# Two gated-DeltaNet heads through one blockwise inverse, in the same tiles and banks

## The chip, the cores and the metric

The kernel runs on one core of a Trainium2 chip. The metric is device time in microseconds (us) of that core, from the start of the program to its end; a time is the median of several executions. A core has a matrix engine (TensorE, PE in the profile, with its weight loads as PEld), a vector engine (VectorE, DVE), a scalar engine (ScalarE, ACT), a general one (GpSimd, POOL) and a queue that issues the DMAs (SyncE, SP). Each takes its instructions in the order in which the program holds them and stops at the first that is not ready.

## What is computed

Two decoder layers over x of shape (1, 512, 1024). Each layer is `x += norm(mixer(norm(x)))`, then `x += norm(ffn(norm(x)))`. The mixer of layer 0 has an mLSTM with 4 heads and a gated DeltaNet (GDN) with 4 heads beside each other; the change touches only the GDN heads. For one head, in chunks of 64 tokens:

```python
kk = jnp.einsum("nbhld,nbhsd->nbhls", kc, kc)
a_mat = jnp.where(strict, bc[..., :, None] * kk * decay, 0.0) + jnp.eye(L)
rhs = jnp.concatenate([vc * bc[..., None], kc * (bc * jnp.exp(G))[..., None]], -1)
sol = lax.linalg.triangular_solve(a_mat, rhs, left_side=True, lower=True, unit_diagonal=True)
u, w = sol[..., :DV], sol[..., DV:]
attn = jnp.einsum("nbhld,nbhsd->nbhls", qc, kc) * decay
def step(state, inp):
    v_new = u_ - w_ @ state
    o = qd_ @ state + attn_ @ v_new
    state = gl_ * state + kd_.T @ v_new
```

q and k are the l2-normed outputs of a depthwise convolution with SiLU on a projection of u, v the same without the norm; the output goes through a norm per head and a gate.

## The kernel before

The 512 tokens stand as four tiles of 128. A matrix product in about full fp32 precision is three matmuls of fp32r halves (`mm3`, lines L188 to L190: high by high, high by low, low by high). A projection of 128 features (`feature_block`) is 8 x 3 such matmuls of 128x512 into one PSUM bank, called pf; a token block (pt) has 256 columns. The weights of a block come by one DMA (raw) and are split into whi (a cast on ACT) and wlo (a subtraction, L101, on DVE or POOL).

PSUM has eight banks, in four groups: pj (3, the projections), mx (2, all the small work of the heads), sc (2, the scans) and po (1). A tile that asks for a bank waits until the last reader of the tile before in that bank is done.

A GDN head (`gdn_head`) runs so. `decay_t` broadcasts a row over the partitions (rowbc) and makes dec; qd is the decayed q. The keys are transposed (kt), ACT squares them with an accumulated sum (`chunk_squares`, L420) for the l2 norm, and DVE makes kbe and kd. Then mt = -(k k^T) times decay and beta, in four tiles of 128x128 (L682). The chunk of 64 tokens gives two 64-row halves of each tile, so that with the four tiles there are eight triangular matrices; the inverse works on the two halves as two 64x64 quadrants of TensorE (`both`). It builds X and its transpose xt from blocks of 1, 2, 4, up to 64 rows: a first run of matmuls (pp, pq, L716 and L717) with a fill for blocks of 2; five levels, each a run of pp (L734), a copy of it to PR on ACT (L736), a run of pe and pet (L740, L741) and two fills on DVE (`copy_predicated`, L708); and a last run (pp, pq, L748, L751, a copy of PR, L753, and pd, L758). ACT puts the result into xtf. After that come wt = kbe times the inverse (L764), the transposes of q (qt) with their squares for the norm of the queries (nq), the scan over the four tiles (vn, S, o) and the head's output (`head_out`). at = k q^T stands behind the first fills, the transposes of v (vt) ahead of level 32.

The heads are called as gdn(0), gdn(1), mlstm(0), gdn(2), gdn(3), mlstm(1); each mlstm takes two heads. Before a head its blocks k, q, v and gate are projected, and the next head's blocks are what TensorE has to do while a chain of small steps is under way. The order on each engine is not that of the code: at build a list scheduler lays all instructions out by modelled costs and writes one fixed sequence for each engine. The program therefore has small steps of a head with projection matmuls (pf, pt) between them.

Of the kernel before, what the change touches and what calls it, by code (L numbers as in the profile page):

```python
# [8 lines left out]
AF = mybir.ActivationFunctionType  # L9
# [9 lines left out]
P = 128  # L19
S = 512  # L20
# [15 lines left out]
def kernel(  # L36
# [409 lines left out]
    def ab_mix(pm, u, load0, pre):  # L446
        w_in = ab_w_in[0]
        wv = w_in.rearrange("(k p) c -> p k c", p=P)
        BUFS = dict(dm=1, mt=1, X=1, PR=1, wt=1, vb=1, v=1, kbe=1, dec=3)
# [21 lines left out]
        gw = small("gw", [P, KD, 16])  # L471
# [31 lines left out]
        first = [piece(fcols(c, 0), V) for c in (2056, 1544, 2568)]  # L503
# [40 lines left out]
        xtfs = [small(f"xtf{i}", [P, S]) for i in range(2)]  # L544
        for x_ in xtfs:
            G.memset(x_, 0.0)

# [12 lines left out]
        e = small("e", [P, NT, 8])  # L560
        stt(e, pf, -1.0, pf, ALU.mult, ALU.max)
        A.activation(out=e, in_=e, func=AF.Exp, scale=-1.0)
        z = small("z", [P, NT, 8])
# [3 lines left out]
        z2 = small("z2", [P, NT, 8])  # L567
        tt(V, z2, z, z, ALU.mult)
        hn = small("hn", [P, NT, 8])
# [81 lines left out]
        def gdn_head(h, k, q, vf, gs):  # L651
            dec, prow = decay_t(4 + h, bg[:, :, 4 + h], True)
            qd = s("qd")
            A.activation(out=qd, in_=prow, func=AF.Exp)
            gl = small("gl", [P, NT], bufs=2)
            V.tensor_copy(gl, v4(qd)[:, :, P - 1])
            tt(V, qd, qd, q, ALU.mult)
            pt = mxt("kt")
            transpose4(pt, k, range(NT))
            ss = col(4, "l2s")  # L660
            chunk_squares(ss, v4(pt))
            v = col(4, "l2v")
            V.tensor_scalar(out=v, in0=ss, scalar1=0.5, scalar2=EPS / 2, op0=ALU.mult, op1=ALU.add)
            rk = rsqrt(v, 4, "l2")
# [3 lines left out]
            ik = col(4, "ik")  # L668
            stt(ik, v, 2.0, rk, ALU.mult, ALU.mult)
            r2 = col(4, "r2")  # L670
            tt(V, r2, rk, rk, ALU.mult)
            dr = small("dr", [P, NT], bufs=2)
            tt(V, dr, r2, beta[:, :, h], ALU.mult)
            dm = s("dm")
            stt(v4(dm), v4(dec), -1.0, bc(dr, P), ALU.mult, ALU.mult)
            kbe = s("kbe")
            tt(V, v4(kbe), v4(pt), bc(eg[:, :, h], P), ALU.mult)
            kd = s("kd")
            tt(V, v4(kd), v4(pt), bc(v4(dec)[:, :, P - 1], P), ALU.mult)
            pmt = mxt("mt")  # L680
            for cs in css:
                T.matmul(pmt[:, cs], lhsT=k[:, cs], rhs=k[:, cs], start=True, stop=True)  # L682

            mt = s("mt")
            tt(V, mt, pmt, dm, ALU.mult)
# [3 lines left out]
            lo, hi = slice(0, 64), slice(64, P)  # L689
            both = ((lo, lo, hi), (hi, hi, lo))  # L690
            xt, xx = (small(n, [P, NT, 64]) for n in ("xt", "X"))
            for x_ in (xt, xx):
                A.copy(out=x_, in_=bm(identc, NT))

            def fill(b, x_, data, t, rows=slice(0, P)):

                def part(ap):
                    return ap.rearrange("p c (n a r) -> p c n a r", a=2, r=b)[:, :, :, t, :]

                if t:  # L700
                    mask = mkt[rows, LEVELS.index(b), :].rearrange("p (n r) -> p n r", r=b)
                elif b == 1:
                    mask = mk1[rows].rearrange("p (n r) -> p n r", r=1)
                else:
                    mask = mk[rows, LEVELS.index(b) - 1, :].rearrange("p (n a r) -> p n a r", a=2, r=b)[:, :, 0, :]
                n = 32 // b
                mask = mask.unsqueeze(1).broadcast_to([mask.shape[0], NT, n, b])
                V.copy_predicated(out=part(x_), mask=mask, data=part(data))  # L708

            def halves_of(ps):  # L710
                return ps[:, : NT * 64].rearrange("p (c n) -> p c n", c=NT)

            pp, pq = (halves_of(mxt(n)) for n in ("pp", "pq"))
            for c in range(NT):
                for rs, cs, os in both:
                    T.matmul(pp[rs, c], lhsT=v4(mt)[rs, c, cs], rhs=identc[rs], start=True, stop=True)  # L716
# [3 lines left out]
            pa = mxt("at")  # L720
            for cs in css:
                T.matmul(pa[:, cs], lhsT=k[:, cs], rhs=q[:, cs], start=True, stop=True)
            at_ = dec
            tt(V, at_, pa, dec, ALU.mult)
            for b in LEVELS[1:-1]:
                if b == 32:
                    pt = mxt("vt")
                    transpose4(pt, vf, range(NT))
                    vb = s("vb")
                    tt(V, v4(vb), v4(pt), bc(ik, P), ALU.mult)  # L730
                pp = halves_of(mxt("pp"))
                for c in range(NT):
                    for rs, cs, os in both:
                        T.matmul(pp[os, c], lhsT=v4(mt)[rs, c, cs], rhs=xx[rs, c], start=True, stop=True)  # L734
                pr = small("PR", [P, NT, 64])
                A.copy(out=pr, in_=pp)  # L736
                pes = [halves_of(mxt(n)) for n in ("pe", "pet")]
                for c in range(NT):
                    for rs, _, os in both:
                        T.matmul(pes[0][rs, c], lhsT=xt[os, c], rhs=pr[os, c], start=True, stop=True)  # L740
                        T.matmul(pes[1][os, c], lhsT=pr[os, c], rhs=xt[os, c], start=True, stop=True)  # L741
                fill(b, xx, pes[0], 0)
                fill(b, xt, pes[1], 1)

            xtf = xtfs[h % 2]
            pp, pq = (halves_of(mxt(n)) for n in ("pp", "pq"))
            for c in range(NT):
                T.matmul(pp[lo, c], lhsT=v4(mt)[lo, c, hi], rhs=xx[lo, c], start=True, stop=True)  # L748
            for c in range(NT):
                for rs, _, os in both:  # L750
                    T.matmul(pq[rs, c], lhsT=identc[os], rhs=xt[os, c], start=True, stop=True)  # L751
            pr = small("PR", [P, NT, 64])
            A.copy(out=pr[lo], in_=pp[lo])  # L753
            for rs, cs, _ in both:
                A.copy(out=v4(xtf)[rs, :, cs], in_=pq[rs])
            pd = halves_of(mxt("pd"))
            for c in range(NT):
                T.matmul(pd[lo, c], lhsT=pr[lo, c], rhs=xt[lo, c], start=True, stop=True)  # L758
            A.copy(out=v4(xtf)[lo, :, hi], in_=pd[lo])
            xt = xtf  # L760

            pw = mxt("wt")
            for cs in css:
                T.matmul(pw[:, cs], lhsT=kbe[:, cs], rhs=xt[:, cs], start=True, stop=True)  # L764
            wt = s("wt")
            A.copy(out=wt, in_=pw)
            pt = mxt("qt")
            transpose4(pt, q, range(NT))

            nq = col(4, "nq")  # L770
            chunk_squares(nq, v4(pt))
            V.tensor_scalar(out=nq, in0=nq, scalar1=EPS, scalar2=0.5 * P * EPS, op0=ALU.add, op1=ALU.mult)

            st = None
            po = bank("po", "o")
            for c, cs in enumerate(css):
                pn = bank("sc", "vn")
                T.matmul(pn[:, :P], lhsT=xt[:, cs], rhs=vb[:, cs], start=True, stop=c == 0)
                if c:
# [470 lines left out]
```

## Time and profile before

| | |
|---|---|
| median of 3 runs | 1356.19 us (1356.08 to 1356.34) |
| the profiled execution | 1356.14 us, span 1354.4 us |
| granted clock of TensorE | 0.998 |
| busy share of the span | PE 98%, PEld 80%, DVE 50%, ACT 45%, POOL 27% |
| DMA | 121.26 MB, mean 90 GB/s |

The span is the time between the first and the last instruction that the profiler recorded. A row of the timeline reads: start, length, engine, line of the kernel, operation, output tile<-input tiles, shape, count, and in brackets the idle time ahead with what ended it. The length of a matmul's row contains the depth of the pipeline, so the rows overlap; what a matmul costs in a sequence is the distance from its start to the start of the next. A matmul on plain fp32 that isn't a transpose has two records (16 records of pp are 8 matmuls).

### The profile page before, as it was taken

The page shows a single profiled execution, that of the slowest core. Times are in us where ns is not written, and L with a number is a line of the kernel's source. Part 1 is how long each engine was busy: PE and PEld are TensorE (multiplying, and loading weights), DVE is VectorE, ACT ScalarE, POOL GpSimd, SP SyncE. Part 2 cuts the span into 40 slices and gives each one's busy share as a digit, 9 for nine tenths or more (in the row PEclk, how much of TensorE's full clock was granted, in tenths as well). Part 3 has the DMA queues.
Part 4 walks back from the last instruction along what each step waited for, and adds up shares of the span by engine and source line. Part 5 has one row for each costly group of instructions (what it writes and reads, how often), then busy time and mean ns, then how long its engine had stood idle before and what let it go on. Part 6 is the DMA issues. An engine that isn't in the chain of part 4 may idle for free.

```text
span 1354.4 us, 20263 instructions
## 1 busy us (share of the span) xinstructions
PE 1324.2 (98%) x7969; PEld 1088.8 (80%) x7969; DVE 680.0 (50%) x1400; ACT 614.9 (45%) x1173; POOL 362.1 (27%) x193
## 2 busy tenths in 40 slices
PE   5999999999999999999999999999999999999997
PEld 5777778778988888888878788878798888888886
DVE  6856586457543333311185775786656333332114
ACT  6844655445443333332265654554544333333222
POOL 0000000000465555544300000000036555554440
PEclk9999999999999999999999999999999999999999
DMA  6512121134333333322224122321233333322211
GB/s 188 132 49 64 36 78 47 49 125 133 95 106 104 94 93 96 106 94 93 95 84 133 63 63 63 93 64 48 73 99 116 103 93 98 104 94 94 94 62 62
DMA packets 165565, 121.26 MB, mean 90 GB/s; under 512 B 9246, under 2 KB 151006, under 8 KB 165470
## 3 DMA queue, kind: packets, MB, share of 16 engines
q1 hardware_dynamic: 165470, 119.96, 28.9%
q8 instruction: 63, 1.03, 0.3%
q14 instruction: 32, 0.26, 0.1%
HBM read 117.85 MB, written 2.10 MB: 89 GB/s over the span
## 4 chain that ended last, share of the span: by engine, by line
PE 86%; DVE 9%; ACT 2%; issue 1%; DMA 1%; SPq 1%; DVEq 0%; ACTq 0%
PE pf L188 17%; PE pf L189 17%; PE pf L190 17%; PE dn L188 6%; PE dn L189 6%; PE dn L190 6%; DVE wlo L101 2%; PE mo L188 1%; PE mo L189 1%; PE mo L190 1%; PE lev L997 1%; DVE un L104 1%; PE pp L734 1%; PE pt L190 1%; PE pt L189 1%
## 5 line engine op out<-in xcount | busy, mean ns | idle before, releaser
L101 POOL TENSOR_TENSOR wlo<-raw,whi 128x1024 fp32r<-128x1024 f32 x122 | 294.3, 2413 | 626.4 <-ACT whi L206 620.3
L188 PE MATMUL pf<-uh,whi 128*128 128x512 f32 (+1 forms) x1168 | 443.7, 380 | 0.0
L189 PE MATMUL pf<-ul,whi 128*128 128x512 f32 (+1 forms) x1168 | 442.6, 379 | 0.4 <-DVE ul L101 0.4
L190 PE MATMUL pf<-uh,wlo 128*128 128x512 f32 (+1 forms) x1168 | 441.8, 378 | 0.0
L206 ACT CAST whi<-raw 128x1024 fp32r<-128x1024 f32 x206 | 215.5, 1048 | 229.7 <-PE pf L189 205.3
L104 DVE SCALAR_TENSOR_TENSOR acc<-pf,fcw,acc 128x511 f32<-128x511 f32 (+1 forms) x176 | 131.5, 749 | 279.8 <-ACT acc L308 277.0
L188 PEld LDWEIGHTS pf<-uh,whi 128*128 128x128 f32 x1168 | 219.8, 188 | 40.2 <-ACT uh L211 0.5
L189 PEld LDWEIGHTS pf<-ul,whi 128*128 128x128 f32 x1168 | 220.0, 188 | 38.5 <-DVE ul L101 0.9
L190 PEld LDWEIGHTS pf<-uh,wlo 128*128 128x128 f32 x1168 | 220.1, 188 | 38.4 <-issue 0.3
L188 PE MATMUL dn<-whi,hh 128*128 128x512 f32 x352 | 137.2, 390 | 0.0
L189 PE MATMUL dn<-wlo,hh 128*128 128x512 f32 x352 | 137.0, 389 | 0.0
L190 PE MATMUL dn<-whi,hl 128*128 128x512 f32 x352 | 137.0, 389 | 0.0
L101 DVE TENSOR_TENSOR wlo<-raw,whi 128x1024 fp32r<-128x1024 f32 (+2 forms) x87 | 107.5, 1236 | 50.8 <-ACT whi L206 45.0
L101 DVE TENSOR_TENSOR hl<-h,hh 128x512 fp32r<-128x512 f32 x44 | 31.6, 718 | 160.3 <-ACT hh L362 160.3
L362 ACT CAST hh<-h 128x512 fp32r<-128x512 f32 x44 | 27.3, 621 | 152.2 <-PE dn L189 131.4
L629 POOL TENSOR_SCALAR_AFFINE_SELECT dec<-dec 128x512 f32<-128x512 f32 x8 | 7.1, 891 | 268.8 <-DVE dec L101 170.4
L188 PEld LDWEIGHTS dn<-whi,hh 128*128 128x128 f32 x352 | 66.1, 188 | 14.2 <-issue 0.5
L189 PEld LDWEIGHTS dn<-wlo,hh 128*128 128x128 f32 x352 | 66.1, 188 | 13.7
L190 PEld LDWEIGHTS dn<-whi,hl 128*128 128x128 f32 x352 | 66.1, 188 | 13.5
L308 ACT ACTIVATE acc<-pf,fcb,fcw 128x512 f32<-128x512 f32 x88 | 67.7, 769 | 8.2 <-POOL sg L101 5.7
L101 POOL TENSOR_TENSOR sg<-sg,acc 128x512 f32<-128x512 f32 x44 | 57.8, 1313 | 30.9 <-ACT sg L339 30.9
L339 ACT ACTIVATE sg<-acc 128x512 f32<-128x512 f32 x44 | 27.8, 632 | 66.7 <-DVE acc L104 66.7
(324 smaller groups left out, 1615.5 us busy)
## 6 DMA issues: line engine op xcount, KB each, us to landing
raw<-in_ffn_w_up_dram SPq DMA_DIRECT2D x88, 512.0 KB, 3.7
raw<-in_ffn_w_down_dram SPq DMA_DIRECT2D x44, 512.0 KB, 3.2
raw<-in_c_w_in_dram SPq DMA_DIRECT2D x32, 512.0 KB, 3.9
raw<-in_ab_w_in_dram SPq DMA_DIRECT2D x26, 512.0 KB, 3.8
gain<-in_norm_gains_dram SPq DMA_DIRECT2D x8, 512.0 KB, 4.9
raw<-in_ab_w_out_dram SPq DMA_DIRECT2D x8, 512.0 KB, 3.9
raw<-in_c_w_out_dram SPq DMA_DIRECT2D x8, 512.0 KB, 3.9
x<-in_x_dram SPq DMA_DIRECT2D x4, 512.0 KB
```

The source lines that it names most:

```text
L101: return eng.tensor_tensor(out=o, in0=a, in1=b, op=op)
L104: V.scalar_tensor_tensor(out=o, in0=a, scalar=s, in1=b, op0=op0, op1=op1, **kw)
L188: T.matmul(ps, lhsT=lh, rhs=rh, start=start, stop=False)
L189: T.matmul(ps, lhsT=lh, rhs=rl, start=False, stop=False)
L190: T.matmul(ps, lhsT=ll, rhs=rh, start=False, stop=stop)
L206: A.copy(out=hv, in_=rv)
L308: A.activation(out=acc, in_=ps, func=AF.Identity, scale=taps[:, K - 1 : K], bias=bias)
L339: A.activation(out=sg, in_=ag, func=AF.Sigmoid)
L362: A.copy(out=hi, in_=hT[k])
L629: G.affine_select(out=v4(d), in_=v4(d), pattern=[[0, NT], [1, P]], compare_op=ALU.is_ge, fill=-BIG, base=0, channel_multiplier=-1,)
L734: T.matmul(pp[os, c], lhsT=v4(mt)[rs, c, cs], rhs=xx[rs, c], start=True, stop=True)
L997: T.matmul(pl4[i * 64 : (i + 1) * 64, c], lhsT=kr[:, c * P + i * 64 : c * P + (i + 1) * 64], rhs=qf[:, :, at : at + 32], start=True, stop= ...
```

## The change

Two heads are taken together (`gdn_pair`, called as gdn(0), mlstm(0), gdn(1), mlstm(1)). Their chunks stand in one tile and one bank: PC = 2 x NT = 8 chunks of 64 columns, 512 in all, where a head had 256. The first run, the levels and the last run go over eight chunks; the copies and fills have twice the width. Both heads' steps ahead of the inverse (decay, kt, squares, kbe, kd, mt) come before it, with one chain of small operations for the l2 norm of both. The inverse is written into mt's tiles (mts) instead of xtf. The transposes and squares of q move to level 8, ahead of its pp; those of v to levels 16 and 32, a head each. The gates are projected behind the inverse (`gates`). The first three pieces of the layer's input weights are k of head 0, k of head 1 and q of head 0, where they were k, q and v of head 0. A few scratch tiles share memory with others. The diff, cut to its core:

```diff
-        BUFS = dict(dm=1, mt=1, X=1, PR=1, wt=1, vb=1, v=1, kbe=1, dec=3)
+        BUFS = dict(wt=1, v=3, dec=3)
...
-        first = [piece(fcols(c, 0), V) for c in (2056, 1544, 2568)]
+        first = [piece(fcols(c, h), V) for c, h in ((2056, 0), (2056, 1), (1544, 0))]
...
-        xtfs = [small(f"xtf{i}", [P, S]) for i in range(2)]
-        for x_ in xtfs:
-            G.memset(x_, 0.0)
...
+        PC = 2 * NT
+        def chunks(ps):
+            return ps.rearrange("p (c n) -> p c n", c=PC)
...
-        def gdn_head(h, k, q, vf, gs):
+        def gdn_pair(j, k, q, vf, gates):
+            heads = (2 * j, 2 * j + 1)
...
+            for a, h in enumerate(heads):
+                dec, prow = decay_t(4 + h, bg[:, :, 4 + h], True)
...
+                transpose4(pt, k[a], range(NT))
+                chunk_squares(ss[:, 4 * a : 4 * a + 4], v4(pt))
...
-            rk = rsqrt(v, 4, "l2")
+            rk = rsqrt(v, 8, "l2")
...
+            mc = [v4(mts[c // NT])[:, c % NT] for c in range(PC)]
...
-            pp, pq = (halves_of(mxt(n)) for n in ("pp", "pq"))
-            for c in range(NT):
+            pp, pq = (chunks(mxt(n)) for n in ("pp", "pq"))
+            for c in range(PC):
                 for rs, cs, os in both:
-                    T.matmul(pp[rs, c], lhsT=v4(mt)[rs, c, cs], rhs=identc[rs], start=True, stop=True)
-                    T.matmul(pq[os, c], lhsT=identc[rs], rhs=v4(mt)[rs, c, cs], start=True, stop=True)
+                    T.matmul(pp[rs, c], lhsT=mc[c][rs, cs], rhs=identc[rs], start=True, stop=True)
+                    T.matmul(pq[os, c], lhsT=identc[rs], rhs=mc[c][rs, cs], start=True, stop=True)
...
             for b in LEVELS[1:-1]:
-                if b == 32:
+                if b == 8:
+                    for a in range(2):
+                        pt = mxt("qt")
+                        transpose4(pt, q[a], range(NT))
+                        chunk_squares(nq[:, 4 * a : 4 * a + 4], v4(pt))
+                if b > 8:
+                    a = len(vbs)
                     pt = mxt("vt")
-                    transpose4(pt, vf, range(NT))
+                    transpose4(pt, vf[a], range(NT))
...
-                pp = halves_of(mxt("pp"))
-                for c in range(NT):
+                pp = chunks(mxt("pp"))
+                for c in range(PC):
...
-            xtf = xtfs[h % 2]
...
-            for rs, cs, _ in both:
-                A.copy(out=v4(xtf)[rs, :, cs], in_=pq[rs])
...
+            for a in range(2):
+                ac = slice(a * NT, (a + 1) * NT)
+                for rs, cs, _ in both:
+                    A.copy(out=v4(mts[a])[rs, :, cs], in_=pq[rs, ac])
+                A.copy(out=v4(mts[a])[lo, :, hi], in_=pd[lo, ac])
+            gss = gates()
+            for a, h in enumerate(heads):
...
         gdn(0)
-        gdn(1)
         params = load_params(cmix)
         mlstm(0)
-        gdn(2)
-        gdn(3)
+        gdn(1)
         mlstm(1)
```

How this moves the instructions is seen in the order that the scheduler wrote. On PE, one level of the inverse: the second head of before (uh, ul, whi and wlo are halves of the projection's operands; x8 and x16 count the matmuls of a row):

```order
L741 MATMUL pet<-xt,PR 64x64
L188 MATMUL pf<-uh,whi 128x512
L189 MATMUL pf<-ul,whi 128x512
L734 MATMUL pp<-X,mt 64x64 x8
L190 MATMUL pf<-uh,wlo 128x512
L188 MATMUL pf<-uh,whi 128x512
L189 MATMUL pf<-ul,whi 128x512
L740 MATMUL pe<-PR,xt 64x64
L741 MATMUL pet<-xt,PR 64x64
```

Between a run of pe and pet and the next pp two wide matmuls stood, and three behind pp. PE, the same place in the first pair after:

```order
L758 MATMUL pet<-xt,PR 64x64
L189 MATMUL pf<-ul,whi 128x512
L190 MATMUL pf<-uh,wlo 128x512
L188 MATMUL pf<-uh,whi 128x512
L751 MATMUL pp<-X,mt 64x64 x16
L189 MATMUL pf<-ul,whi 128x512
L190 MATMUL pf<-uh,wlo 128x512
L188 MATMUL pf<-uh,whi 128x512
L189 MATMUL pf<-ul,whi 128x512
L757 MATMUL pe<-PR,xt 64x64
L758 MATMUL pet<-xt,PR 64x64
```

The run holds sixteen pp, and three and four wide matmuls stand around it. On PE, the first run of the first head of before begins so:

```order
L189 MATMUL pf<-ul,whi 128x512
L190 MATMUL pf<-uh,wlo 128x512
L716 MATMUL pp<-identc,mt 64x64
L717 MATMUL pq<-mt,identc 64x64
L716 MATMUL pp<-identc,mt 64x64
L717 MATMUL pq<-mt,identc 64x64
```

There pp and pq took turns from the start. On PE, the first run of the first pair after:

```order
L189 MATMUL pf<-ul,whi 128x512
L190 MATMUL pf<-uh,wlo 128x512
L722 MATMUL pp<-identc,mt 64x64 x7
L723 MATMUL pq<-mt,identc 64x64 x7
L722 MATMUL pp<-identc,mt 64x64
L723 MATMUL pq<-mt,identc 64x64
```

Seven of each now stand by themselves before they take turns. On PE, the transposes of both heads' queries at level 8 of the second pair after, where pt is a token block with 256 columns:

```order
L188 MATMUL pt<-whi,uh 128x256
L216 MATMUL qt<-ident,q 128x128 x8
L189 MATMUL pt<-wlo,uh 128x256
L190 MATMUL pt<-whi,ul 128x256
L188 MATMUL pt<-whi,uh 128x256
L189 MATMUL pt<-wlo,uh 128x256
L190 MATMUL pt<-whi,ul 128x256
L188 MATMUL pt<-whi,uh 128x256
L189 MATMUL pt<-wlo,uh 128x256
L190 MATMUL pt<-whi,ul 128x256
L188 MATMUL pt<-whi,uh 128x256
L751 MATMUL pp<-X,mt 64x64 x16
```

The eight transposes come between two levels, nine matmuls of pt ahead of the next pp. On ACT, the squares of the same transposes in the first pair after (a copy of PR belongs to each level; the casts are weights of later blocks):

```order
L753 COPY PR<-pp 128x512
L420 ACTIVATE junk,nq<-qt 128x128 x4
L206 CAST whi<-raw 128x1024
L420 ACTIVATE junk,nq<-qt 128x128
L306 ACTIVATE q<-pf,cmix 128x512
L420 ACTIVATE junk,nq<-qt 128x128
L753 COPY PR<-pp 128x512
L420 ACTIVATE junk,nq<-qt 128x128 x2
```

Six of the eight squares stand ahead of that level's copy and two behind it. On DVE, ahead of the first fill of before (dr is a column of factors, dm the decay with it, gl the last column of qd):

```order
L104 SCALAR_TENSOR_TENSOR dm<-dec,dr 128x512
L656 COPY gl<-qd 128x4
L101 TENSOR_TENSOR kd<-kt,dec 128x512
L101 TENSOR_TENSOR qd<-qd,q 128x512
L101 TENSOR_TENSOR mt<-mt,dm 128x512
L104 SCALAR_TENSOR_TENSOR k<-pf,cmix,k 128x511
L101 TENSOR_TENSOR wlo<-raw,whi 128x1024
L708 COPY_PREDICATED X<-mk_501,pp 128x128
```

A step of a convolution and a weight split stood between mt and the fill. DVE, the same place in the first pair after (sig stands for dm, gs the gate of a GDN head):

```order
L101 TENSOR_TENSOR dr<-r_810,beta 128x8
L104 SCALAR_TENSOR_TENSOR sig<-dec,dr 128x512 x2
L101 TENSOR_TENSOR mt<-mt,sig 128x512 x2
L104 SCALAR_TENSOR_TENSOR gs<-pf,cmix,sig 128x512
L665 COPY_PREDICATED X<-mk_501,pp 128x256
L665 COPY_PREDICATED xt<-maskst,pq 128x256
```

Both heads' mt stand there one behind the other, with gs between them and the fills of twice the width.

More of the change, by code (lines that the diff above doesn't have):

```diff
@@ L648, in ab_mix @@
         css = [slice(c * P, (c + 1) * P) for c in range(NT)]
-        def gdn_head(h, k, q, vf, gs):
[L652 to L662, printed above, removed]
+        lo, hi = slice(0, 64), slice(64, P)
@@ L675, in gdn_head @@
[L675 to L689, printed above, removed]
@@ L690, in gdn_head @@
-            both = ((lo, lo, hi), (hi, hi, lo))
-            xt, xx = (small(n, [P, NT, 64]) for n in ("xt", "X"))
-            for x_ in (xt, xx):
[L693 to L708, printed above, removed]
@@ L710, in halves_of @@
-            def halves_of(ps):
-                return ps[:, : NT * 64].rearrange("p (c n) -> p c n", c=NT)
-            pp, pq = (halves_of(mxt(n)) for n in ("pp", "pq"))
-            for c in range(NT):
+            dr = small("dr", [P, 2, NT], bufs=2)
+            tt(
+                V, dr, r2.rearrange("p (a c) -> p a c", a=2),
+                beta[:, :, heads[0] : heads[1] + 1].rearrange("p c a -> p a c"), ALU.mult,
+            )
+            mts = []
+            for a in range(2):
+                dm = s("sig")
+                stt(v4(dm), v4(decs[a]), -1.0, bc(dr[:, a], P), ALU.mult, ALU.mult)
+                pmt = mxt("mt")
+                for cs in css:
+                    T.matmul(pmt[:, cs], lhsT=k[a][:, cs], rhs=k[a][:, cs], start=True, stop=True)
+                mt = s("mt")
+                tt(V, mt, pmt, dm, ALU.mult)
+                mts.append(mt)
@@ L733, in gdn_head @@
                     for rs, cs, os in both:
-                        T.matmul(pp[os, c], lhsT=v4(mt)[rs, c, cs], rhs=xx[rs, c], start=True, stop=True)
-                pr = small("PR", [P, NT, 64])
+                        T.matmul(pp[os, c], lhsT=mc[c][rs, cs], rhs=xx[rs, c], start=True, stop=True)
+                pr = small("PR", [P, PC, 64])
                 A.copy(out=pr, in_=pp)
-                pes = [halves_of(mxt(n)) for n in ("pe", "pet")]
-                for c in range(NT):
+                pes = [chunks(mxt(n)) for n in ("pe", "pet")]
@@ L739, in gdn_head @@
+                for c in range(PC):
                     for rs, _, os in both:
@@ L743, in gdn_head @@
                 fill(b, xt, pes[1], 1)
-            xtf = xtfs[h % 2]
[L746 to L749, printed above, removed]
+            pp, pq = (chunks(mxt(n)) for n in ("pp", "pq"))
+            for c in range(PC):
+                T.matmul(pp[lo, c], lhsT=mc[c][lo, hi], rhs=xx[lo, c], start=True, stop=True)
+            for c in range(PC):
@@ L758, in gdn_head @@
                 T.matmul(pd[lo, c], lhsT=pr[lo, c], rhs=xt[lo, c], start=True, stop=True)
[L759 to L771, printed above, removed]
```

154 lines of the change are left out of this document (94 added, 60 removed).

## The prediction, made before the changed kernel ran

> **What bounds the kernel now.** I read the page first, then the busy time by stretches, the waits of TensorE, and last the timeline of TensorE inside the inverse.
>
> ```profile
> PE 1324.2 (98%) x7969; PEld 1088.8 (80%) x7969; DVE 680.0 (50%) x1400; ACT 614.9 (45%) x1173; POOL 362.1 (27%) x193
> PE 86%; DVE 9%; ACT 2%; issue 1%; DMA 1%; SPq 1%; DVEq 0%; ACTq 0%
> ```
>
> TensorE (PE) is busy for 98% of the span and carries 86% of the chain that ended last. The stretches (columns: from and to, length, then the busy us of PE, PEld, DVE, ACT, POOL) say where the rest is:
>
> ```profile
> 0.00:12.00 12.00, 0.11 (x1) 0.14 (x2) 3.16 (x13) 6.94 (x16) 2.92 (x17) 1.00 0.82 231
> 12.00:22.00 10.00, 8.24 (x48) 6.87 (x49) 9.09 (x26) 9.62 (x24) 0.00 (x0) 1.00 0.88 259
> 60.00:285.00 225.00, 222.68 (x2258) 175.27 (x2256) 144.23 (x350) 114.73 (x277) 7.09 (x8) 1.00 0.19 58
> ```
>
> Of 30 us without PE work, 13.6 us lie in the first 22 us. In the 225 us from 60 to 285, which hold the four inverses, PE has 2.3 us of idle time, at the full clock (1.00). The waits of PE in that stretch (total, times, longest) are these:
>
> ```profile
> PE pd L758 <- ACT PR L753: 0.9, 4, 0.2
> ...
> PE pp L734 <- DVE X L708: 0.2, 1, 0.2
> PE pp L748 <- DVE X L708: 0.2, 1, 0.2
> PE mt L682 <- ACT qd L654: 0.2, 1, 0.2
> ```
>
> So the chain through the inverse's levels (matmul, copy, matmul, two fills, next level) is long, but projection matmuls cover it. Fewer rounds of that chain are worth nothing by themselves. What counts is whether PE needs less time for the same matmuls. "Busy" can hide that, so I read the timeline of one level of the second head (start, length, engine, line, op, tiles, size, count):
>
> ```profile
> 121.17 0.40 PE L190 MATMUL pf<-uh,wlo 128*128 128x512 f32 x1
> 121.50 0.68 PE L734 MATMUL pp<-X,mt 64*64 64x64 f32 x16
> 122.11 0.50 PE L188 MATMUL pf<-uh,whi 128*128 128x512 f32 x1
> 122.45 0.39 PE L189 MATMUL pf<-ul,whi 128*128 128x512 f32 x1
> 122.68 0.40 PE L190 MATMUL pf<-uh,wlo 128*128 128x512 f32 x1
> 123.00 0.27 PE L740 MATMUL pe<-PR,xt 64*64 64x64 f32 x1
> ...
> 123.48 0.22 PE L741 MATMUL pet<-xt,PR 64*64 64x64 f32 x1
> 123.63 0.50 PE L188 MATMUL pf<-uh,whi 128*128 128x512 f32 x1
> 123.96 0.40 PE L189 MATMUL pf<-ul,whi 128*128 128x512 f32 x1
> ```
>
> Two wide matmuls (128x512) in a row start 0.23 us apart (122.45 to 122.68). Next to a run of small matmuls (64*64) they don't: the run starts 0.33 after the wide one, the next wide one takes 0.33 or 0.34 to hand over. From 121.17 to 122.45 there are 1.28 us; less two wide steps (0.46) a run of pp costs 0.82. From 122.68 to 123.96 it is 1.28 again, 0.82 for a run of pe and pet with twice as many records (32 for 16). Price of a run and price of its matmuls are thus different things.
>
> **The change part by part.** The program's order holds the same 6804 matmuls before and after, of the same sizes; none is added or removed. What differs on PE is order and grouping.
>
> *Fewer, longer runs.* Counted in the order: before, a head has one run of pp and pq, five levels of two runs, and a last run (pp, pq, pd), 12 in all, 48 for four heads, and one more since the first head's first pe and pet stand apart: 49. After, a pair has the same 12 with twice the matmuls, and the second pair's first run is cut once: 25. So 24 runs go. What is a run's fixed part? Two rows bound it.
>
> ```profile
> 252.29 0.68 PE L758 MATMUL pd<-xt,PR 64*64 64x64 f32 x8 [0.21 <-ACT PR L753]
> 277.88 0.40 PE L188 MATMUL mo<-whi,yhi 128*128 128x512 f32 x1
> 278.21 1.09 PE L830 MATMUL ms<-q,k 64*64 64x128 f32 x16
> 279.23 0.50 PE L189 MATMUL mo<-wlo,yhi 128*128 128x512 f32 x1
> 279.56 0.39 PE L190 MATMUL mo<-whi,ylo 128*128 128x512 f32 x1
> ```
>
> Four chunks on one quadrant (pd, 8 records, each 0.22 long as the row at 123.48) take 0.68, so 0.46 from the first start to the last: that is the work of four chunks, and the fixed part is 0.82 - 0.46 = 0.36. The run of ms has the records of pp with twice the columns: 277.88 to 279.56 is 1.68, less 0.46 is 1.22; doubling the work added 0.40, which leaves a fixed part of 0.42. I take 0.36, because here the number of matmuls doubles, as in the first way. 24 x 0.36 = **-8.6 us** (-10.1 by the other end). Eight runs before and five after follow transposes or at without a wide matmul between, and so lack one slow hand-over (0.33 for 0.23); that is +0.3, but at and qt come in four groups for eight, which gives about as much back.
>
> At this place a rule speaks against the change. In before, pp's lower and upper row groups already write one bank, and 16 records took the 0.68 us that 8 records of pd took on one quadrant: two row groups ran at once on one bank. The Trainium skill, TensorEngine Tiling (Array Packing), Restrictions and Gotchas, says that different row tiles cannot access the same PSUM bank simultaneously. The trace of before disagrees with that, at 256 columns a bank; that a bank holding both heads' 512 columns behaves the same, no run here shows yet, so the rule stays a rival with a small chance below.
>
> *A worse order in two runs.* The first pair's first run starts with 7 pp and then 7 pq, where before pp and pq alternate; the second pair's has 8 pp by themselves and then 8 pq. Alternating, four quadrants work; alone, two. Seven of each take 7 steps for 3.5, eight of each 8 for 4; a step of one chunk is 0.46 / 4 = 0.115. So 7.5 x 0.115 = **+0.9 us** (0 if the hardware were free to overlap them, nothing worse).
>
> *The wait of pd.* PE waits for the copy of PR four times, 0.9 us in all. After, twice as many pq lie between (16 in twos, 8 x 0.115 = 0.92 where 0.46 lay), and the copy grows from 64x256 to 64x512; its two ends are in these rows (count | busy, mean ns):
>
> ```profile
> L736 ACT COPY PR<-pp 128x256 f32<-128x256 f32 x20 | 7.5, 373 | 33.4 <-PE pp L734 33.4
> L766 ACT COPY wt<-wt 128x512 f32<-128x512 f32 x4 | 2.3, 581 | 2.1 <-PE wt L764 2.1
> L708 DVE COPY_PREDICATED X<-masks,pe 128x128 f32<-128x128 uint8 x20 | 6.5, 326 | 22.1 <-PE pet L741 21.9 <-PE pe L740 0.2
> ```
>
> A 512-wide copy takes 0.58, 0.21 more, and the cover grows by 0.46: the wait goes, **-0.9 us** (0 at the other end).
>
> *The levels themselves.* Here the filler counts. In the first pair it is wide matmuls, four between pp and pe where three stood, three between pet and pp where two stood. In the second pair the order has matmuls of 256 columns (pt), six and four; their pace, and the slack of the same level of before, are in these rows (PE's timeline, then ACT's and DVE's):
>
> ```profile
> 226.11 0.28 PE L189 MATMUL pt<-wlo,uh 128*128 128x256 f32 x1
> 226.23 0.28 PE L190 MATMUL pt<-whi,ul 128*128 128x256 f32 x1
> ...
> 122.29 0.37 ACT L736 COPY PR<-pp 128x256 f32<-128x256 f32 x1 [0.96 <-PE pp L734]
> ...
> 123.75 0.29 DVE L708 COPY_PREDICATED X<-masks,pe 128x128 f32<-128x128 uint8 x1 [1.53 <-PE pet L741]
> ```
>
> At 0.12 each, six are 0.72 and four 0.48, where three and two wide ones gave 0.68 and 0.45: about the same cover. The copy ended at 122.66 and pe began at 123.00: 0.34 of slack for 0.21 more copy. The fill ended at 124.04 and the next pp began at 124.29 (123.96 + 0.33): 0.25 of slack; a fill of twice the width is 0.16 longer by the 56% that the copies show, 0.29 if all of it scales. So 0, ends 0 and +1.0 (0.1 at each of ten places).
>
> *The prelude of a pair.* Here is the new danger. Before a pair's first pp, DVE has the convolutions of six blocks in its queue instead of three, and both heads' decay, qd, kbe, kd and mt. In before this place looks so (one stretch of DVE, its timeline, and the first pp):
>
> ```profile
> 41.72:70.98 29.26, 28.20 (x167) 22.05 (x165) 27.68 (x69) 21.22 (x34) 0.64 (x1) 1.00 0.39 108
> ...
> 67.99 0.68 DVE L101 TENSOR_TENSOR qd<-qd,q 128x512 f32<-128x512 f32 x1
> 68.59 0.69 DVE L101 TENSOR_TENSOR mt<-mt,dm 128x512 f32<-128x512 f32 x1
> 69.19 0.74 DVE L104 SCALAR_TENSOR_TENSOR k<-pf,cmix,k 128x511 f32<-128x511 f32 x1
> 69.84 1.22 DVE L101 TENSOR_TENSOR wlo<-raw,whi 128x1024 fp32r<-128x1024 f32 x1
> 70.98 0.45 DVE L708 COPY_PREDICATED X<-mk,pp 128x128 f32<-128x128 uint8 x1
> ```
>
> ```profile
> 69.53 0.27 PE L716 MATMUL pp<-identc,mt 64*64 64x64 f32 x1
> ```
>
> From the first k convolution (41.72) to the first fill DVE is busy 27.7 of 29.3 us. After, the order adds three convolutions (each 3 x 0.65 + 0.6, by the starts above: 7.7), three weight splits (1.14 each: 3.4) and six 512-wide operations (0.6 each: 3.6), 14.7 us; with idle in proportion (29.3 / 27.7) 15.5, so DVE reaches the fill near 86.5. PE reaches the first pp later too: 72 more wide matmuls (213 for 141 in the order, 0.23 each: 16.6), the second head's row broadcast (0.23), and about 1 us for its transposes and k k^T: 69.53 + 17.8 = 87.3. So PE and DVE meet within a microsecond, as they did before. What follows there: gs is queued behind mt on DVE, gs frees a projection bank, and the next wide block on PE waits for that bank, so a late DVE holds up the filler as well. In before this place and the next pp cost 0.2 once each over four heads (rows L682 and L734), 0.4 in all. I take twice that, since twice as much is queued: **+0.4 us** net (-0.4 with no wait at all; +5 if DVE is some 2.5 late in each pair).
>
> *The queries' norms amid the inverse.* qt moves from behind wt to level 8: the eight transposes of both heads take both mx banks there, and the next pp, pe and pet need those banks. Eight squares on ACT have to read them first, at 0.40 from start to start, as the same squares of kt show (ACT's timeline):
>
> ```profile
> 60.58 0.28 ACT L420 ACTIVATE junk<-kt 128x128 bf16<-128x128 f32 x1 [1.45 <-PE kt L216]
> ...
> 60.98 0.28 ACT L420 ACTIVATE junk<-kt 128x128 bf16<-128x128 f32 x1
> ```
>
> In the second pair all eight (3.2) stand ahead of the copy of PR (0.58), so that ends near 3.8; PE has the second four transposes (0.4), nine pt (1.1), the run of pp (1.3) and seven pt (0.8) until 3.6: 0.2 of waiting. In the first pair ACT's order has a cast and a convolution between the squares and two of them behind the copy, so the second bank comes free 0.8 after PR does; PE starts with seven pe alone, and seven pet follow: 7 x 0.46 / 8 = 0.4 lost to half-used quadrants, and little waiting. **+0.6 us** for both (0 and +1.5, if each pair waits 0.5 more).
>
> *Covered edits, taken at nothing.* 54 DVE instructions, 6 ACT table loads and two GpSimd memsets fewer: none is on PE's path in 60 to 285. The gates' two blocks stand behind the inverse in the code, but near its first run in the order (DVE's gs), and are filler there as the gate was. SP has as many DMAs in the same order of kinds, with k of head 1 and q of head 0 as second and third piece. At the start DVE takes one weight split before a half's ul instead of behind it: at nothing, within one split's 1.14 either way.
>
> Sum: -8.6 + 0.9 - 0.9 + 0.4 + 0.6 = -7.6 us. The profiled execution took 1356.14 (span 1354.4), 0.05 under the median of the three runs, so the forecast is **1348.5 us**.
>
> **The rivals.**
> - *The cost goes with the matmuls, not with the runs* (0.05). Then merging saves nothing, and +0.9 - 0.9 + 0.4 + 0.6 leaves 1357.1. Against it: pe and pet with 32 records cost what pp does with 16, and ms with twice the columns added 0.40, not 0.82.
> - *DVE becomes the bound in the preludes and eats most of it* (0.08). PE waits 2 to 4 us before each pair's first pp: 1352 to 1356. For it: 95% busy in that stretch already. Against: PE comes later by as much as DVE.
> - *The same, so far that the change loses* (0.05). One mechanism: mt is late, gs behind it holds the bank, PE stands. It decides from 7.6 + 2.7 = 10.3 us, 5.2 a pair: DVE's 44.8 us (86.5 - 41.7) would have to stretch by 12% more where idle was 6% of its work before. At 6 a pair: 1360.5.
> - *Row groups take turns in a full bank* (0.02): each of some 20 runs on four quadrants would need its work, 2 x 0.46, a second time, +18.4: 1366.9. By the skill's rule above; the rows of before speak against it.
>
> **How the numbers follow.** The forecast with its own spread (-11 to -4: the other fixed part and no waits at one end, -10.1 - 0.9 - 0.4 = -11.4; +1.0 for fills, +1.0 more at the norms and two waits of about 1 at the other) has 0.80. The range 1345.0 to 1353.5 takes nearly all of the low end and reaches into the case where DVE eats part. 0.2% is about what a measurement of this kernel can tell from no change, 2.7 us: faster means under 1353.5. Faster 0.80 + 0.06 of the second rival = 0.86; same 0.05 + 0.02 = 0.07; slower 0.05 + 0.02 = 0.07.
>
> **What would show it.** Runs of small matmuls that cost about 1.28 us (0.36 + 2 x 0.46) where two cost 1.64 before; 25 of them; no wait of PE for PR; wide matmuls, dn and layer 1 unchanged; the mixer's output matmuls starting some 8 us earlier. Wrong would be: PE waiting over 2 us at the first pp of a pair, or a run of 16 pp taking more than 1.4 us.

## The result, and the profile after

The changed kernel takes 1349.13 us (median of 6 runs, 1348.88 to 1350.14) against 1356.13 us for the kernel before (median of 6): a ratio of 0.995 with a 95% interval of 0.9937 to 0.9963. The forecast was 1348.5 us in a range of 1345.0 to 1353.5.

The page of the kernel after, first two lines of its busy times (engine, us, share of the span, instructions):

```profile
span 1347.5 us, 20168 instructions
PE 1316.8 (98%) x7969; PEld 1090.7 (81%) x7969; DVE 675.4 (50%) x1346; ACT 606.3 (45%) x1151; POOL 361.7 (27%) x191
```

TensorE still is busy for 98%, with the same 7969 records, but for 1316.8 us where it had 1324.2. So the share of busy time tells nothing here: the same matmuls became cheaper. All of it lies ahead of the mixer's output. The matmuls of that part (mo from yhi) are one row in a view by tile (count, shortest, median and longest ns, first and last start), here of before and of after:

```profile
L188 PE MATMUL mo<-whi,yhi x128: 387/389/499, 274.4 to 980.2; 128*128 128x512 f32 x128
...
L188 PE MATMUL mo<-whi,yhi x128: 387/389/501, 267.5 to 973.2; 128*128 128x512 f32 x128
```

The first started 6.9 us earlier and the last 7.0, as much as the span is shorter; what lies between and behind them did not change.

One level of the first pair, in PE's timeline (start, length, engine, line, op, tiles, shape, count):

```profile
93.55 0.39 PE L190 MATMUL pf<-uh,wlo 128*128 128x512 f32 x1
93.87 1.15 PE L751 MATMUL pp<-X,mt 64*64 64x64 f32 x32
94.95 0.50 PE L188 MATMUL pf<-uh,whi 128*128 128x512 f32 x1
95.29 0.40 PE L189 MATMUL pf<-ul,whi 128*128 128x512 f32 x1
```

From 93.55 to 95.29 are 1.74 us; less two wide steps (0.46), a run of pp with twice the records costs 1.28, where two cost 1.64 before. That is the number the prediction named.

The waits of PE from 60 to 285 us (total, times, longest) are these after:

```profile
PE pp L764 <- DVE X L665: 0.9, 1, 0.9
PE vt L216 <- DVE X L665: 0.6, 1, 0.6
PE pt L188 <- ACT vaug L492: 0.5, 1, 0.5
PE pp L751 <- DVE X L665: 0.5, 2, 0.3
PE wt L784 <- ACT mt L777: 0.3, 1, 0.3
```

The wait of pd for PR, 0.9 us in four places, is gone. Waits for the fill of X stand in its place, 2.0 us in four places where before had two of under 0.2. Two of them have the same cause, seen on DVE in the second pair:

```profile
229.46 1.23 DVE L101 TENSOR_TENSOR wlo<-raw,whi 128x1024 fp32r<-128x1024 f32 x1 [2.59 <-ACT whi L206]
230.61 0.43 DVE L665 COPY_PREDICATED X<-masks,pe 128x256 f32<-128x256 uint8 x1
```

The last pe and pet were done near 229.3, but DVE, after waiting 2.59 us for the cast of whi on ACT, began a weight split of 1.23 us at 229.46; the fill stands behind it in DVE's order, came at 230.61, and the next pp at 231.09.

### The profile page after: what moved, and what is told of

Its sections match the earlier page's. It is cut to its first block, busy times and chain, and to the rows that moved or that the text cites. A ratio compares the mean times of both kernels' runs of the same rounds, so it can differ in the third digit from the quotient of the medians.

```text
span 1347.5 us, 20168 instructions
## 1 busy us (share of the span) xinstructions
PE 1316.8 (98%) x7969; PEld 1090.7 (81%) x7969; DVE 675.4 (50%) x1346; ACT 606.3 (45%) x1151; POOL 361.7 (27%) x191
## 4 chain that ended last, share of the span: by engine, by line
PE 86%; DVE 8%; ACT 3%; issue 1%; DMA 1%; SPq 0%; POOL 0%; DVEq 0%; ACTq 0%; POOLq 0%
PE pf L188 17%; PE pf L189 17%; PE pf L190 17%; PE dn L188 6%; PE dn L189 6%; PE dn L190 6%; DVE wlo L101 2%; PE mo L188 1%; PE mo L189 1%; PE mo L190 1%; PE lev L1011 1%; PE pt L190 1%; PE pt L189 1%; PE pt L188 1%; DVE un L104 1%
```

## The experiments

All twelve are edits of the kernel after. They stand in three series (e1 to e4, e5 to e8, e9 to e12), each with runs of the kernel before, whose median moved between 1355.7 and 1356.1. The kernel after was not run again, so a few tenths of a microsecond between series say little.

**The start.** In the first 22 us a difference stands that the prediction had put at nothing. On PE, the first token block of after:

```profile
14.01 0.59 PE L188 MATMUL pt<-whi,uh 128*128 128x272 f32 x1 [0.16 <-ACT uh L211]
...
16.88 0.43 PE L188 MATMUL pt<-whi,uh 128*128 128x272 f32 x1
17.11 0.43 PE L189 MATMUL pt<-wlo,uh 128*128 128x272 f32 x1
...
18.07 0.29 PE L189 MATMUL pt<-wlo,uh 128*128 128x272 f32 x1
18.20 0.29 PE L190 MATMUL pt<-whi,ul 128*128 128x272 f32 x1
```

The first pt came 0.36 later than before (13.65), and the matmuls were 0.23 apart until 17.5, then 0.13; in the profile of before the slow pace ended at 15.5. ACT sets X and xt to the identity there, now 512 columns each, ahead of the first weight casts. Two runs take that out of the way. The first gives the copies to GpSimd:

```diff
-                A.copy(out=x_, in_=bm(identc, PC))
+                G.tensor_copy(x_, bm(identc, PC))
```

> The kernel after, with the two copies that set X and xt to the identity taken from ACT to GpSimd. Theory (the start): in the kernel after these copies are twice as wide (0.60 and 0.62 us for 0.40) and stand on ACT ahead of the first weight casts and of uh, so the first pt comes 0.36 us later than before, PE pauses at another moment, and its half pace (0.23 us from one pt to the next) lasts until 17.5 us where it ended at 15.4: 1.3 us in all at the first 24 projection matmuls. With the copies gone from ACT the first pt starts at 13.6 or earlier, the half pace ends near 15.5, and the time falls by 0.5 to 1.3 us, to about 1348.2. Rival (the start costs nothing, as the prediction had it, and what differs there is made up later): within 0.3 us of the kernel after, 1349.1.

Measured 1349.27 us: no gain, and a later first pt (14.43). GpSimd's and DVE's timelines of this run say why:

```profile
10.82 0.61 POOL L718 COPY xt<-identc 128x512 f32<-128x512 f32 x1 [8.19 <-DVE identc L541]
11.37 0.61 POOL L718 COPY X<-identc 128x512 f32<-128x512 f32 x1
...
10.88 0.56 DVE L104 SCALAR_TENSOR_TENSOR tk_r<-tk_q,tk_y 128x1 f32<-128x1 f32 x1
11.47 1.71 DVE L104 SCALAR_TENSOR_TENSOR un<-x,tk_r,gain 128x512 f32<-128x512 f32 x2
```

An operation on one column took 0.56 us while the copy of GpSimd ran (0.16 in the kernel after), and un, on which the first transposes wait, came later. The edit brought a new wait of its own, so it told nothing on the theory. The second run moves only the time of the copies: the tiles of xt and X first serve as scratch memory.

```diff
-        gw = small("PR", [P, 2 * NT * 64])[...]
+        gw = small("xt", [P, 2 * NT * 64])[...]
-        scratch = s("wt")
+        scratch = small("X", [P, 2 * NT * 64])
```

> The kernel after, with the tiles of X and xt first lent to small scratch data of the start, so that ACT sets them to the identity only later and not ahead of the first weight casts (nothing goes to GpSimd, unlike e1_init). Theory (the start): the first pt starts at 13.6 us or earlier, where the kernel after had 14.01; the half pace of PE ends nearer to the 15.4 of the kernel before than to 17.5; 0.5 to 1.3 us less than the kernel after, 1347.8 to 1348.6. Rival (the length of the half pace is set by something else, such as when PE pauses, and the copies only shift the first pt): 0.4 us less at most, or a start as long as before.

Measured 1348.43 us (1348.13 to 1348.81), 0.7 less; the first pt at 13.65 again, as before, and the slow pace until 17.0. So the copies cost the first pt its 0.36 us. The end of the slow pace moved less than the theory said: it isn't set by them alone (see the last section). From the 24th projection matmul to the first matmul of the mixer's output, e9 and after take the same 228.9 us: all of its gain lies at the start.

**The order of the first runs.** In after the first run of the first pair is this:

```profile
87.90 0.39 PE L190 MATMUL pf<-uh,wlo 128*128 128x512 f32 x1
88.23 0.66 PE L722 MATMUL pp<-identc,mt 64*64 64x64 f32 x14
88.73 0.50 PE L723 MATMUL pq<-mt,identc 64*64 64x64 f32 x9
...
89.81 0.50 PE L188 MATMUL pf<-uh,whi 128*128 128x512 f32 x1
90.15 0.39 PE L189 MATMUL pf<-ul,whi 128*128 128x512 f32 x1
```

2.25 less 0.46 is 1.79, half a microsecond above a level's run. The run e2 gives pq a bank of the scans:

```diff
-            pp, pq = (chunks(mxt(n)) for n in ("pp", "pq"))
+            pp, pq = chunks(mxt("pp")), chunks(bank("sc", "pq"))
```

> The kernel after, with pq of a pair's first run in a bank of the scans (sc) and not of mx, so that the order has pp and pq in turns from the start. Theory (half-used quadrants): the first runs, 1.80 us in the first pair and 0.89 + 1.37 in the second, become 1.30 each: 1.0 to 1.5 us less, 1347.7 to 1348.1. Rival (the first run hangs on what reaches PE through mt and DVE, and its length is only waiting in another form): the run is short, PE waits as long at the next pp, and the time stays at 1349.1.

Measured 1346.88 us, 2.2 less than after (1.8, if each is taken against the kernel before in its own series), more than the 1.0 to 1.5 of the theory. In both pairs pp and pq take turns, and the order changed with them: at follows the first run directly, and the second pair's fills no longer fall behind a split (the waits of 0.62 and 0.86 are gone; in the first pair one of 0.99 stands where 0.31 stood, and a new one of 0.30). So half-used quadrants cost about what the prediction gave them; the rest of this gain is a luckier order, not the quadrants.

**The splits ahead of the fills.** The run e3 moves the weight splits of the second mLSTM pair from DVE to GpSimd:

```diff
-            k = conv_silu(feature_block(fcols(256, j), u, V), ...)
+            e_ = G if j else V
+            k = conv_silu(feature_block(fcols(256, j), u, e_), ...)
```

(the same for q and the gates)

> The kernel after, with the weight splits (wlo) of the blocks k, q and both gates of the second mlstm pair on GpSimd and not on DVE. Theory (late fills): the waits of 0.62 us (vt for the fill of X at 225.5) and 0.86 us (pp for X at 231.1) come from a split of 1.23 us that stands on DVE ahead of the fill; without it both go, 1.0 to 1.5 us less, about 1347.8. Rival: GpSimd takes 2.4 us for such a split, as in the rows of the feed-forward part, so wlo comes late for the projection, PE waits there instead, and the time is 1349.1 or above; or the fills are late for another reason and the waits stay.

Measured 1354.99 us: 5.9 more than after. One of the two waits was gone (vt), the other stayed, and three new ones came, none of which the expectation had named. PE's waits in this run, then GpSimd's and DVE's timelines at one of them:

```profile
PE pp L722 <- DVE mt L101: 2.4, 1, 2.4
PE yt L216 <- DVE yn L101: 2.1, 2, 1.9
PE mt L707 <- DVE l2v L687: 1.2, 1, 1.2
```

```profile
200.22 2.40 POOL L101 TENSOR_TENSOR wlo<-raw,whi 128x1024 fp32r<-128x1024 f32 x1 [4.69 <-issue]
...
200.29 2.35 DVE L101 TENSOR_TENSOR l_q<-l_q,l2v 128x8 f32<-128x8 f32 x1
202.67 0.17 DVE L104 SCALAR_TENSOR_TENSOR l_y<-l_q,l_y 128x8 f32<-128x8 f32 x1
```

A DVE operation on eight columns, 0.17 us beside it, took 2.35 as it began 0.07 after a split on GpSimd: it stood until the split was over. That is one of the chain to mt, and PE waited 2.4 us for mt. The waits cost more than their length: the granted clock of TensorE fell to 0.50 at about 205.6 us and stayed there until 209, behind the wait for mt, which by these figures is another 1.7 us (an estimate). So the time of this run says nothing against the reading of the two waits, and nothing for it beyond the one that went.

> The kernel after with the three edits of the runs e1_init, e2_alternate and e3_pool_splits together. Theory: they are three terms in three places (start, first runs, second pair's fills) and add up: 2.5 to 4.3 us less than the kernel after, 1345 to 1346.6. Rival: each removed wait uncovers the next one behind it, so that the three together give no more than the best of them, 1347.6 to 1348.2.

Measured 1353.69 us, for the same reason: the waits for mt (2.37) and yn (1.87) stand in its trace as well, and the granted clock is at 0.50 for about 3.4 us behind each. Whether three terms add up was then tried without GpSimd, with the edits of e2 and e9:

> The edits of e2_alternate and e9_late_copies together. Theory (two places, nothing shared): e2_alternate's 1346.9 less what e9_late_copies gains on the kernel after, 0.5 to 1.3: 1345.6 to 1346.4. Rival (the first run's wait for mt takes back what the start gives, since DVE carries the prelude and PE only arrives earlier): 1346.9.

Measured 1346.16 us (1345.69 to 1346.52), 0.7 below e2 as e9 is below after: the two add up. The traces say the same: from the 24th projection matmul to the mixer's output e10 takes 225.5 us and e2 225.7, so the late copies change nothing there. This is the fastest version, at 0.9926 of the kernel before (0.9914 to 0.9939).

**The price of a run.** In e5 each run of the levels is cut by one matmul of 256 columns that leaves no trace in the result; in e6 the same matmuls stand beside the wide ones.

```diff
                 for c in range(PC):
+                    if c == NT:
+                        T.matmul(pp[:, NT:], lhsT=rows[:, :P], rhs=rows[:, :256], start=True, stop=True)
```

(in e5; in e6 it stands ahead of the loop; the same for pe)

> The kernel after, with every run of pp and of pe and pet in the five levels of both pairs cut in two by one matmul of 128x256 amid it (its result is overwritten by the second half): the same small matmuls in 20 more runs, and 20 more matmuls of 128x256 of about 0.12 us. Theory (a run has a fixed part of 0.36 us, whatever it holds): 20 x (0.36 + 0.12) = 9.6 us more than the kernel after, about 1358.7, and 7.2 us above the run e6_ahead_of_runs. Rival (the gain came from the engines beside PE, or from waits, and not from the number of runs): 20 x 0.12 = 2.4 us more, 1351.5, the same as e6_ahead_of_runs.

> The control of e5_split_runs: the same 20 matmuls of 128x256 ahead of the runs, beside the wide matmuls that stand there anyway, so that no run is cut. Both theories: 20 x 0.12 = 2.4 us more than the kernel after, about 1351.5; somewhat less where one of them fills a wait of PE.

Measured 1357.32 and 1352.91 us. The rival (no difference) is out: 4.4 us lie between them. The theory's 7.2 was too much, and the traces say where the difference went. The cut itself costs nearly what was expected, in e5's timeline of PE:

```profile
93.20 0.39 PE L190 MATMUL pf<-uh,wlo 128*128 128x512 f32 x1
93.52 0.68 PE L753 MATMUL pp<-X,mt 64*64 64x64 f32 x16
94.13 0.39 PE L751 MATMUL pp<-rows 128*128 128x256 f32 x1
94.44 0.68 PE L753 MATMUL pp<-X,mt 64*64 64x64 f32 x16
95.06 0.50 PE L188 MATMUL pf<-uh,whi 128*128 128x512 f32 x1
95.39 0.39 PE L189 MATMUL pf<-ul,whi 128*128 128x512 f32 x1
```

2.19 from 93.20 to 95.39, less 0.46 and 0.12 for the added matmul, is 1.61 where one run cost 1.28: 0.33 for one more run, 6.6 for twenty. But the control was not free: its order cut the mLSTM's runs of ms from two into five,

```profile
143.76 1.06 PE L845 MATMUL ms<-q,k 64*64 64x128 f32 x14
146.09 0.43 PE L845 MATMUL ms<-q,k 64*64 64x128 f32 x2
146.88 0.43 PE L845 MATMUL ms<-q,k 64*64 64x128 f32 x2
148.59 0.65 PE L845 MATMUL ms<-q,k 64*64 64x128 f32 x8
149.82 0.65 PE L845 MATMUL ms<-q,k 64*64 64x128 f32 x6
```

which is three runs more, about 1.0 at that price. From an added matmul to a run of pp it took 0.29 to 0.32 us, 0.1 more than from a pt (0.21), in nine places: 0.9. With 0.6 for a price of 0.33 where 0.36 was taken, 0.3 of the missing 2.8 stay untraced.

**The norms.** The run e7 puts qt and the squares back behind wt, a head at a time.

> The kernel after, with the transposes of the queries and their squares back behind wt, a head at a time, as in the kernel before. Theory (the norms amid the inverse cost what the prediction gave, 0.6 us): the run of pe and pet at level 8 of the first pair falls from 1.81 to 1.30 us, the two waits for banks there (0.06 and 0.15) go; four groups of transposes for two give back 0.2 to 0.4, so 0.2 to 0.5 less, about 1348.8. Rival (the squares are covered in either place, the long run is only a wait shown in another way): within 0.2 us of 1349.1; or the squares lie in the way of the scans, 0.3 to 1 more.

Measured 1349.59 us: no gain. In after the level's run of pe and pet costs 1.80,

```profile
107.14 0.40 PE L188 MATMUL pf<-uh,whi 128*128 128x512 f32 x1
107.47 0.67 PE L757 MATMUL pe<-PR,xt 64*64 64x64 f32 x14
107.99 0.50 PE L758 MATMUL pet<-xt,PR 64*64 64x64 f32 x9
...
109.06 0.50 PE L189 MATMUL pf<-ul,whi 128*128 128x512 f32 x1
109.40 0.39 PE L190 MATMUL pf<-uh,wlo 128*128 128x512 f32 x1
```

half a microsecond above the others, and with two waits of 0.06 and 0.15 that makes 0.7. In e7 the run is at 1.30 and the two waits are gone; the late fills cost 1.6 for 2.0 (vt waits 0.51 in the first pair where it waited 0.62 in the second, the last pp 0.62 for 0.86). From the 24th projection matmul to the mixer's output its trace is 1.0 us shorter than that of after (227.9 for 228.9), but the medians show no gain. On top of e10 it was tried again:

> As e10_alternate_late, with the queries' norms back behind wt as in e7_norms_back. Theory (in the trace of e7_norms_back the stretch from the 72nd projection matmul to the first output matmul was 1.0 us shorter than in the kernel after, 216.3 for 217.3): 0.5 to 1.0 less than e10_alternate_late. Rival (the norms are worth nothing in either place, as the medians of e7_norms_back and of the kernel after say): the same as e10_alternate_late within 0.4.

Measured 1346.21 us, for 1346.16 without, and the same stretch is 1.2 us longer here than in e10 (226.7 for 225.5). What one order gained the other lost; the rival (worth nothing in either place) holds as far as these medians can tell.

**How near DVE is to the bound.** The run e8 adds three operations a head on DVE ahead of mt:

```diff
+                for _ in range(3):
+                    tt(V, dm, dm, dm, ALU.max)
```

> The kernel after, with three more operations of 128x512 on DVE for each head ahead of mt (about 0.6 us each, 3.7 us a pair; they change no value), in the place where the prediction's rival had DVE as the bound. Theory (the order is laid out anew, projection matmuls stand ahead of the first pp for as long as DVE needs, and these are covered): under 1 us more than the kernel after, 1349 to 1350. Rival (DVE bounds the prelude: mt late, the gate behind it holds a projection bank, PE stands): 3 us or more a pair, 6 to 7.5 us more, 1355 to 1356.6.

Measured 1354.11 us, 5.0 more than after: nearer to the rival than to the theory. PE's first wait in its trace:

```profile
PE pp L724 <- DVE mt L101: 2.8, 1, 2.8
```

Of 3.7 us added in the first pair PE waited for 2.8; 0.9 was covered, 0.7 of it by three wide matmuls that the new order put ahead of the first pp. In the second pair the new order put more pt ahead of the first pp and there was no such wait. The profiled execution took 1355.41 us, 6.2 more than that of after, and the wait alone isn't that much. Behind it the granted clock was 0.50 from about 91.6 us to 98.4, where PE had work from 92.4 on: by these figures another 3 us (an estimate). And the half pace at the start lasted until 19.9 us for 17.5, so that the 24th projection matmul came 1.0 later. So the wait that the rival names cost about its own length again in clock, in this execution.

**Two row groups on one bank.** The run e12 gives the two row groups of pp a bank each.

```diff
-                pp = chunks(mxt("pp"))
+                pps = [chunks(mxt("pp")), chunks(bank("sc", "pph"))]
...
+                for i, (rs, cs, os) in enumerate(both):
+                    A.copy(out=pr[os], in_=pps[i][os])
```

> The kernel after, with the two row groups of a level's pp in two banks (one of mx, one of the scans) and PR copied in two halves. Only the length of a run of 16 pp counts here, from its first start to its last. Theory (two row groups write one bank at the same time): 0.93 us as in the kernel after, where both write one bank. Rival (row groups take turns in one bank): apart they no longer do, and the run falls to about 0.46 us.

It ran once, and only the length of a run is read, by the first and the last records of one level:

```profile
98.06 0.27 PE L751 MATMUL pp<-X,mt 64*64 64x64 f32 x1
98.07 0.27 PE L751 MATMUL pph<-X,mt 64*64 64x64 f32 x1
...
99.00 0.22 PE L751 MATMUL pph<-X,mt 64*64 64x64 f32 x1
```

0.94 from the first start to the last, as in one bank (0.93 in after). The granted clock of this one execution was 0.948, where after had 0.999; the rival's fall to half is far outside what that can hide, a few hundredths are not. So sharing a bank costs next to nothing here, with 512 columns filled. The rule of the Trainium skill that the prediction weighed (TensorEngine Tiling (Array Packing), Restrictions and Gotchas: different row tiles cannot access the same bank simultaneously) doesn't show in these runs.

## Why the prediction was right, point by point

| step | forecast | read in the traces |
|---|---|---|
| 24 runs fewer | -8.6 | -8.6 (49 runs before, 25 after, 0.36 each; 0.33 where a run is cut in e5) |
| order of the first runs | +0.9 | +0.9 (0.5 in the first pair, 0.4 in the second) |
| wait of pd | -0.9 | -0.9 |
| the levels themselves | 0, at most +1.0 | +1.7 (2.0 of waits for fills, 0.3 before) |
| prelude of a pair | +0.4 | -0.1 (0.7 of waits for 0.8) |
| queries' norms | +0.6 | +0.7 |
| start | 0, 1.14 either way | +0.9 |
| other small groups | 0 | -1.1 (48.95 us for 50.02, with half of the hand-overs that they share) |
| sum | -7.6 | -6.5 |

The measured change is -7.0 (medians) and -6.9 (profiles); 0.4 to 0.5 of gain is not in the table. A place for it can be read: two runs of before, at 120.05 and 195.22 us, began with pe alone and cost 0.99 and 1.11 where the others cost 0.83, 0.4 together, and after has no such run beside the one at level 8. The first row is a count times a price, but the whole bears it out: from the 24th projection matmul on, all runs of the inverse with half of the hand-overs they share with other groups, waits left out, take 36.3 us for 44.1. The mechanism was right. The forecast lay only 0.6 below the measured time because sizes missed to either side, the levels and the start up, the prelude and the small groups down; that they nearly met is luck.

*The levels* were outside their bounds. The step had the right slack (0.25 us ahead of pp) and nearly the right fill at most levels (0.43 for 0.29, 48% longer where 56% was taken; at the first level 0.72 for 0.45, and in the second pair that alone makes a wait of 0.17), but it took for granted that DVE is free when pe and pet end. In two places a weight split of 1.23 us stood ahead, in a third the end of a convolution (0.3). Before had one such case: the wait for X at L748 among the rows of the prediction comes from a split that began at 249.62, ahead of a fill at 250.76. The fixed order of DVE was there to read; the step should have followed, level by level, what stands ahead of each fill.

*The start* was called covered. The copies of the identity, which the change made wider, were not looked at: they run at 10.7 us, 80 us before their use, in the one stretch where ACT is what PE waits for. By the 24th projection matmul after was 1.3 us late (38.6 for 37.3), and got 0.4 back by shorter waits until 54 us; only the 0.36 at the first pt are shown to be the copies' doing.

*The other small groups* were said to give back what the lost direct runs cost; they gave more. By the distances of starts the matmuls into at, in two groups for four, took 3.7 us for 4.4, and qt 1.6 for 1.8; that the grouping is the cause fits this, but no run tested it.

*Rivals.* That the cost goes with the matmuls is refuted by e5 and e6, and that row groups take turns by e12. That DVE bounds the prelude did not happen, but the margin was next to nothing. The step had DVE at the first fill near 86.5 us and PE at the first pp at 87.3; in after DVE was through with what stands ahead of that fill at 89.5, and PE began at 88.2. There the first pp of the first pair starts 0.15 us after DVE has ended the first mt (88.08), the same distance as in e8, where PE stood waiting for it. So its small chance was set by a thinner margin than the forecast said. On the mechanism of a run the Trainium skill (TensorEngine Tiling (Array Packing), Tiling Modes, Key Properties) says that a change of the tiling mode drains TensorE; the traces here agree, with a price of about 0.34 us for going in and out.

## What to carry to other kernels

A stretch that shows 98% busy can still shrink: price small matmuls by the distance of starts across a whole run, including both hand-overs, and merge runs where one bank and one copy can hold both. Then read, on each engine that feeds those runs, what stands ahead of each short step in the fixed order, since a long background operation there costs more than the step itself grew. Before moving work to an idle engine, look whether it stops the engine that it is meant to relieve. And keep TensorE from standing for two microseconds: what follows can run at half the clock for several more, as in e3 and e8.

## What the runs showed of the hardware that was not expected

GpSimd stops DVE. In e3 a DVE operation of 0.17 us took 2.35, and one of 0.68 took 2.77, each while a split of 2.4 us ran on GpSimd. The Trainium skill (SBUF — State Buffer, SBUF: two separate sides) says that a DVE operation with two inputs in SBUF and a GpSimd operation that reads SBUF exclude each other for a whole instruction; the traces agree, and the prediction had no step to which it applied.

PE starts at half pace, and for how long differs. Its first work began at 11.9 us in nearly all profiles, but matmuls of 272 columns were 0.23 apart until 15.5 us (before), 17.0 (e9, e10), 17.5 (after), 19.5 (e2) and about 20 (e6, e8); a microsecond of it costs about 0.45, since the same matmuls are 0.126 apart afterwards. The clock column of the profile shows 1.00 there. The Trainium skill (TensorE: Matmul & The Clock Gate, What's actually happening) describes a free-running window whose phase decides when the full rate begins; that the length differs from run to run agrees with that, but the half a microsecond to either side that it gives doesn't: here the shortest and the longest lie 4.6 us apart, and no run here separates phase from the short pauses of PE. It makes single profiles differ by a microsecond or more with nothing changed, so the parts of under a microsecond above rest on rows, not on times.

A wait can halve the clock. In e3, e4 and e8 the granted clock fell from 1.00 to 0.50 within half a microsecond of PE's resuming from a wait of 2.4 us (e3, e4), and 0.8 before it resumed from one of 2.8 (e8). It stayed there for 3.4 us in e3 and e4 and for 6.8 in e8. After a wait of 1.87 it fell in e4 and did not in e3. In before, after, e2 and e10, where no wait from 25 us to the mixer's output is longer than 1.0, it stayed at 1.00 there.
